# Image to columns on one core: all 72 plane copies on VectorE, none on ScalarE

## Chip, cores and metric

One core of a Trainium2 chip (trn2). The metric is the device time of one execution in microseconds (us), lower is better. Each kernel was run several times; a run is fast or slow, and only fast runs are compared.

## The reference

`x` is 16 x 64 x 32 x 32 in fp32, the window 3 x 3. For each of the 30 x 30 positions the patch of 64 x 3 x 3 values becomes a column:

```python
cols = np.zeros((batch, c * kernel_size * kernel_size, h_out * w_out), dtype=np.float32)
for b in range(batch):
    col_idx = 0
    for i in range(h_out):
        for j in range(w_out):
            patch = x[b, :, i:i + kernel_size, j:j + kernel_size].copy()
            cols[b, :, col_idx] = patch.ravel()
            col_idx += 1
```

No arithmetic is done: 4.19 MB go in and 33.18 MB come out, each input value in up to nine shifted copies.

## The kernel before

Each of 128 partitions holds 8 channels (CPP = 8) of one image. Three loads bring them in; for each channel nine copies of 30 x 30 elements, one for each shift (ki, kj), build the output in SBUF; five stores take it out: channel 0, channel 1, then pairs 2-3, 4-5, 6-7. The tile of a pair has two buffers, so pair 4-5 waits until the stores of channels 0 and 1 have landed (31.85 us; VectorE's copies start at 31.97), and pair 6-7 until that of pair 2-3 has (50.97; 51.09). Of every five copies two go to ScalarE.

```python
# (cut: views, pools, and the load helper on the SP queue)
    cuts = [0, H, 200, CPP * H]
    first = load(nc.sync, cuts[0], cuts[1])
    bulk = load(nc.sync, cuts[1], cuts[2])
    load(nc.sync, cuts[2], cuts[3])

    on_act = (False, True, False, True, False)
    n = 0
    for c in range(0, CPP, 2):
        out_tile = out_pool.tile([P, 2, KK, HO, WO], x.dtype, name="out_tile")
        for s in range(2):
            for kk in range(KK):
                ki, kj = divmod(kk, K)
                src = in_tile[:, c + s, ki : ki + HO, kj : kj + WO]
                dst = out_tile[:, s, kk]
                if on_act[n % len(on_act)]:
                    nc.scalar.copy(out=dst, in_=src)
                else:
                    nc.vector.tensor_copy(out=dst, in_=src)
                n += 1
            if c == 0:
                st = nc.sync.dma_start(
                    out=out_v[:, s],
                    in_=out_tile[:, s].rearrange("p kk i j -> p (kk i j)"),
                )
                if s == 0:

                    tc.add_manual_dep(
                        st.ins,
                        bulk.ins.name,
                        mybir.DependencyInfo(
                            mybir.DependencyClass.Sync, mybir.DependencyReason.DATA
                        ),
                        reason="the store follows the bulk of the loads",
                    )
        if c > 0:
            nc.sync.dma_start(
                out=out_v[:, c : c + 2].rearrange("p c n -> p (c n)"),
                in_=out_tile.rearrange("p c kk i j -> p (c kk i j)"),
            )
```

(After this the first load is moved ahead of the start barrier, in both kernels alike.)

Of the kernel before, what the change touches and what calls it, by code (L numbers as in the profile page):

```python
# [1 line left out]

# [3 lines left out]


def _im2col(ctx, tc, x, K, out):


    nc = tc.nc
    P = nc.NUM_PARTITIONS

    B, C, H, W = x.shape
    HO = H - K + 1
    WO = W - K + 1
    KK = K * K
    assert out.shape == (B, C * KK, HO * WO)
    CPP = B * C // P
    assert CPP * P == B * C and C % CPP == 0 and CPP % 4 == 0  # L20

    x_v = x.rearrange("b (cp c2) h w -> (b cp) (c2 h w)", c2=CPP)
    out_v = out.rearrange("b (cp c2 kk) n -> (b cp) c2 (kk n)", c2=CPP, kk=KK)

    in_pool = ctx.enter_context(tc.tile_pool(name="in_pool", bufs=1))
    out_pool = ctx.enter_context(tc.tile_pool(name="out_pool", bufs=2))

    ctx.enter_context(tc.manual_schedule())

    in_tile = in_pool.tile([P, CPP, H, W], x.dtype, name="in_tile")  # L30
    in_flat = in_tile.rearrange("p c h w -> p (c h w)")

    def load(queue, r0, r1):

        return queue.dma_start(
            out=in_flat[:, r0 * W : r1 * W], in_=x_v[:, r0 * W : r1 * W]
        )

    cuts = [0, H, 200, CPP * H]
    first = load(nc.sync, cuts[0], cuts[1])  # L40
    bulk = load(nc.sync, cuts[1], cuts[2])
    load(nc.sync, cuts[2], cuts[3])


    on_act = (False, True, False, True, False)
    n = 0
    for c in range(0, CPP, 2):
        out_tile = out_pool.tile([P, 2, KK, HO, WO], x.dtype, name="out_tile")
        for s in range(2):
            for kk in range(KK):  # L50
                ki, kj = divmod(kk, K)
                src = in_tile[:, c + s, ki : ki + HO, kj : kj + WO]
                dst = out_tile[:, s, kk]
                if on_act[n % len(on_act)]:
                    nc.scalar.copy(out=dst, in_=src)  # L55
                else:
                    nc.vector.tensor_copy(out=dst, in_=src)  # L57
                n += 1
            if c == 0:
                st = nc.sync.dma_start(  # L60
                    out=out_v[:, s],
# [17 lines that stand above are left out]
    return first  # L79


def kernel(
    tc: tile.TileContext,
    x: bass.AP,
    kernel_size: bass.AP,
    out: bass.AP,
):
    with ExitStack() as ctx:
        first = _im2col(ctx, tc, x, int(kernel_size), out)


    tc.close()
    tc.compile()  # L93
    blocks = tc.nc.main_func.blocks
    load = first.ins
    home = next(b for b in blocks if any(i.name == load.name for i in b.instructions))
    home.instructions = [i for i in home.instructions if i.name != load.name]
    head = list(blocks[0].instructions)
    at = next(
        k  # L100
        for k, i in enumerate(head)
        if i.engine == load.engine and type(i).__name__ == "InstDrain"
    )
    head.insert(at, load)
    blocks[0].instructions = head


# [1 line left out]
_INS = ['x', 'kernel_size']  # L109
_OUTS = [((16, 576, 900), 'float32')]  # L110

_NUMBERS = {'kernel_size': 3}


# [26 lines left out]
```

## Time and profile before

| | before |
|---|---|
| time, median of 3 runs at first | 91.44 us (91.39 to 91.49) |
| span of the profiled run (that run took 91.84 us) | 90.1 us |
| VectorE busy / ScalarE busy | 23.5 us / 26.2 us |
| DMA queue, share of 16 engines' time | 97.0% |

Read it as a kernel bound by its transfers: both copy engines are idle three quarters of the time, and the DMA queue is not. The prediction below shows the lines behind this table.

### The profile page before, as it was taken

The numbers are of one execution on the slowest core, as the hardware profiler recorded it, in microseconds if no ns is written. First come the engines' busy times: TensorE is split into PE (matmuls) and PEld (weight loads), VectorE is DVE, ScalarE is ACT, GpSimd is POOL, SyncE is SP. The second block draws the span as 40 slices with busy tenths as digits, with TensorE's granted clock in tenths as the row PEclk, the third lists the DMA queues.
The fourth block names the chain that finished last, engine by engine and source line by source line (L and its number), as shares of the span: only waits on it lengthen the run. The fifth ranks groups of instructions, "written<-read, shape, count | busy, mean of one in ns | idle before, by whom it ended". The sixth has DMA issues, their size and how long they took to land.

```text
span 90.1 us, 140 instructions
## 1 busy us (share of the span) xinstructions
DVE 23.5 (26%) x43; ACT 26.2 (29%) x30; POOL 0.2 (0%) x4
## 2 busy tenths in 40 slices
DVE  0380399970000089600000399300000000000000
ACT  5391399940000089920000399300000000000000
POOL 0000000000000000000000000000000000000000
DMA  5999899999599999993799999999999999947990
GB/s 129 486 382 449 360 518 446 460 460 446 259 460 460 691 460 432 460 432 173 345 460 460 460 460 460 460 460 460 460 460 460 460 432 460 403 201 345 460 460 0
DMA packets 1152, 37.37 MB, mean 415 GB/s; under 512 B 128, under 2 KB 128, under 8 KB 384
## 3 DMA queue, kind: packets, MB, share of 16 engines
q1 hardware_dynamic: 1152, 37.37, 97.0%
HBM read 4.19 MB, written 33.18 MB: 415 GB/s over the span
## 4 chain that ended last, share of the span: by engine, by line
DMA 45%; DVE 16%; DVEq 1%; issue 0%; SPq 0%
DMA out_dram<-out_tile 35%; DVE out_tile L57 16%; DMA in_tile<-in_x_dram 11%; DVEq L93 1%; DVEq L57 0%; SPq L75 0%
## 5 line engine op out<-in xcount | busy, mean ns | idle before, releaser
L55 ACT COPY out_tile<-in_tile 128x900 f32<-128x900 f32 x29 | 24.9, 938 | 30.1 <-DMA out_dram<-out_tile 25.3
L57 DVE COPY out_tile<-in_tile 128x900 f32<-128x900 f32 x43 | 23.5, 624 | 33.6 <-DMA out_dram<-out_tile 26.0
L55 ACT ACT_TABLE_LOAD x1 | 1.3, 1283 | 0.8 <-PEq L122 0.8
L122 POOL MEMSET const-bfloat16-1.0<- 128x1 bf16 x1 | 0.1, 102 | 0.0
L122 POOL MEMSET const-uint8-127<- 128x1 uint8 x1 | 0.1, 102 | 0.0
L122 POOL MEMSET const-float32-0.0<- 128x1 f32 x1 | 0.1, 99 | 0.2 <-issue 0.2
L122 POOL MEMSET const-float32-1.0<- 128x1 f32 x1 | 0.1, 99 | 0.0
## 6 DMA issues: line engine op xcount, KB each, us to landing
out_dram<-out_tile SPq DMA_DIRECT2D x3, 8100.0 KB, 31.3
out_dram<-out_tile SPq DMA_DIRECT2D x2, 4050.0 KB, 14.9
in_tile<-in_x_dram SPq DMA_DIRECT2D x1, 2688.0 KB, 9.6
in_tile<-in_x_dram SPq DMA_DIRECT2D x1, 896.0 KB, 11.4
in_tile<-in_x_dram SPq DMA_DIRECT2D x1, 512.0 KB, 3.6
```

Source lines behind the costliest of these rows:

```text
L55: nc.scalar.copy(out=dst, in_=src)
L57: nc.vector.tensor_copy(out=dst, in_=src)
L93: tc.compile()
L122: nc = _bacc.Bacc("TRN2", target_bir_lowering=False, num_devices=1)
```

## The change

The intent is a simpler program: VectorE alone does all the copies, so that ScalarE, with its table load (1.28 us in the page), is not used at all. The price is a VectorE that works longer and stores that are issued later.

```diff
--- before.py
+++ after.py
@@ -41,21 +41,15 @@
     bulk = load(nc.sync, cuts[1], cuts[2])
     load(nc.sync, cuts[2], cuts[3])
 
-
-    on_act = (False, True, False, True, False)
-    n = 0
     for c in range(0, CPP, 2):
         out_tile = out_pool.tile([P, 2, KK, HO, WO], x.dtype, name="out_tile")
         for s in range(2):
             for kk in range(KK):
                 ki, kj = divmod(kk, K)
-                src = in_tile[:, c + s, ki : ki + HO, kj : kj + WO]
-                dst = out_tile[:, s, kk]
-                if on_act[n % len(on_act)]:
-                    nc.scalar.copy(out=dst, in_=src)
-                else:
-                    nc.vector.tensor_copy(out=dst, in_=src)
-                n += 1
+                nc.vector.tensor_copy(
+                    out=out_tile[:, s, kk],
+                    in_=in_tile[:, c + s, ki : ki + HO, kj : kj + WO],
+                )
             if c == 0:
                 st = nc.sync.dma_start(
                     out=out_v[:, s],
```

## The prediction

With the comparison goes the reason why the stores could not run faster: 434 GB/s is what they ran at, not a ceiling that was shown, so "does not permit" means at that rate. Against contention the measured intervals of 19.1 to 19.2 us remain. The "some 1.2 us" from issue to first bytes is an estimate from one load: issued at 0.00, its first packet starts at 1.01 and the sixteenth at 1.35. The 938 ns under the rivals are one ScalarE copy in the page (mean of 29); the "at most 0.1 to 0.2 us" there is a guess of mine that nothing above works out. The 31.9 us before which the store issued at 19.74 "could not begin moving" are the landing on the slowest DMA engine: that store's first packet starts at 30.76, and the store ahead lands on its 16 engines from 31.15 to 31.85; so it began to move up to 1.1 us earlier than the sentence says.

> **What bounds the kernel now.** I began with the busy shares and the DMA queue of the page:
>
> ```profile
> DVE 23.5 (26%) x43; ACT 26.2 (29%) x30; POOL 0.2 (0%) x4
> ...
> q1 hardware_dynamic: 1152, 37.37, 97.0%
> ```
>
> VectorE (DVE) and ScalarE (ACT) each work about a quarter of the 90.1 us span; the single DMA queue moves 37.37 MB and its packets fill 97.0% of what 16 DMA engines have in that span. No copy engine is near its limit; the transfer of 4.19 MB in and 33.18 MB out nearly is. A share is only an average, so next I looked for moments at which the DMA queue had nothing to do because a copy was late. For that I need issue and landing of each store. The groups of DMA issues and the timeline give them:
>
> ```profile
> out_dram<-out_tile SPq DMA_DIRECT2D x3, 8100.0 KB, 31.3
> out_dram<-out_tile SPq DMA_DIRECT2D x2, 4050.0 KB, 14.9
> ...
> DMA to landing us min/median/max: 11.7/31.2/32.1
> ```
>
> ```profile
> 3.61 3.48 ACT L55 COPY out_tile<-in_tile 128x900 f32<-128x900 f32 x4 [1.54 <-DMA in_tile<-in_x_dram]
> 3.61 2.78 DVE L57 COPY out_tile<-in_tile 128x900 f32<-128x900 f32 x5 [3.61 <-DMA in_tile<-in_x_dram]
> 10.43 8.54 ACT L55 COPY out_tile<-in_tile 128x900 f32<-128x900 f32 x10 [3.35 <-DMA in_tile<-in_x_dram]
> 10.43 9.23 DVE L57 COPY out_tile<-in_tile 128x900 f32<-128x900 f32 x17 [4.04 <-DMA in_tile<-in_x_dram]
> 10.50 3.67 SPq L60 DMA_DIRECT2D out_dram<-out_tile  x2
> 19.74 0.33 SPq L75 DMA_DIRECT2D out_dram<-out_tile  x1
> ...
> 31.97 5.47 DVE L57 COPY out_tile<-in_tile 128x900 f32<-128x900 f32 x10 [12.31 <-DMA out_dram<-out_tile]
> 38.82 18.68 SPq L75 DMA_DIRECT2D out_dram<-out_tile  x2
> 51.07 6.01 ACT L55 COPY out_tile<-in_tile 128x900 f32<-128x900 f32 x7 [12.28 <-DMA out_dram<-out_tile]
> 51.09 6.01 DVE L57 COPY out_tile<-in_tile 128x900 f32<-128x900 f32 x11 [13.66 <-DMA out_dram<-out_tile]
> ```
>
> (Each row: start, duration, engine; in brackets the idle time before and what ended it.) The five stores go out at 10.50, 13.82, 19.74, 38.82 and 57.17 us. With the latencies 11.7 and 18.0 for the two single-channel stores, and 31.2, 31.3 and 32.1 for the three of two channels, they land at 22.2, 31.9, 51.0, 70.1 and 89.3. A store of 8.29 MB therefore lands every 19.1 us, that is 8.29 / 19.1 = 434 GB/s, although it spends over 31 us "in flight": the first 12 or so of those it stands behind the store before. The last load is issued at 1.18 and lands 11.4 later, at 12.6; five stores at that rate need 33.18 MB / 434 GB/s = 76.5 us, and 12.6 + 76.5 = 89.1 against 89.3 seen. The store stream has no hole of any size from 12.6 us on. The remaining 0.8 us to 90.1 is the end of the program.
>
> One view misleads here. The chain that ended last gives DVE 16% of the span:
>
> ```profile
> 10.43 9.24 DVE out_tile L57 x17
> ...
> 19.74 31.24 DMA out_dram<-out_tile
> ...
> 51.09 0.63 DVE out_tile L57
> ```
>
> It follows the last compute instruction back (its list ends at 57.10), and calls the 17 copies before the store at 19.74 part of the path. But that store could not begin moving before the one ahead of it landed at 31.9. Those copies are hidden.
>
> [...] The stretches between landings agree: 31.9 to 51.0 holds 6.9 us of copies on both engines and took 19.1 us, 51.0 to 70.1 holds 6.4 us and took 19.1, and 70.1 to 89.3 holds none and took 19.2.
>
> **The change, part by part.** It removes 29 ScalarE copies (24.9 us busy) and the table load (1.3 us), and adds 29 copies to VectorE. The compiled order shows nothing else: the same three loads and five stores on SP with the same buffer waits, less the wait for ScalarE; VectorE has 72 copies in the order of the code.
>
> VectorE's pace comes from the timeline: 17 copies take 9.23 us, and with 0.624 for the first the other 16 take (9.23 - 0.624)/16 = 0.538 each; the group of 10 gives (5.47 - 0.624)/9 = 0.538 too. So consecutive copies overlap a little, and n copies in a row take 0.624 + (n - 1) x 0.538: 4.93 us for the 9 of one channel, 9.77 for the 18 of a pair, 14.61 for 27. I take the starts from before, since they are set by loads and landings, and add:
>
> - Channel 0, from 3.61: done at 8.54 (before 7.09). Its store waits for the bulk load at 10.43 anyway: issued at 10.50, unmoved, with 1.9 us to spare.
> - Channel 1, from 10.43: done at 15.36, so its store goes out at about 15.4 instead of 13.82. The store ahead lands at 22.2. The first load shows some 1.2 us between issue and the first bytes (issued at 0.00, no DMA activity before 1.0), so anything issued by 21.0 leaves no hole: 5.6 us to spare.
> - Channels 2 and 3, straight after: done at 10.43 + 14.61 = 25.04 (before 19.7). Needed by 31.9 - 1.2 = 30.7: 5.6 us to spare.
> - Channels 4 and 5, when the first buffer is free at 31.97: done at 41.74 (before 38.8). Needed by 49.8: 8 us to spare.
> - Channels 6 and 7, from 51.09: done at 60.86 (before 57.1). Needed by 68.9: 8 us to spare.
>
> So copies of 29 x 0.538 = 15.6 us more on VectorE make four of five stores 1.6 to 5.3 us later at issue, and none later at landing. The sum on the path is 0. On the other side the table load (0.79 to 2.07) ended before the first data at 3.61, and the dropped semaphore wait is 17 ns in SP's record for each store; both were off the path, so the saving is 0 as well. VectorE ends up busy 4.93 + 14.61 + 2 x 9.77 = 39.1 us, 43% of the span.
>
> **The rivals.**
> *VectorE becomes the bound.* For it: it loses all help and its work grows by two thirds. Against it: a pair of channels takes 9.77 us and the DMA queue 19.1 us to drain one; a copy would have to take (19.1 - 1.2)/18 = 1.0 us before the queue ran dry in the steady part. If the copies nevertheless took 938 ns apiece with no overlap, channels 1 to 3 would end at 10.43 + 27 x 0.938 = 35.8 and leave a hole of about 5 us: 96.5 us. The 624 ns of 43 copies, 619 to 630, speak plainly against it.
> *The start gets later.* The beginning is where there is least slack: channel 0 ends 1.45 us later. Were the bulk load's landing not the gate, this would move everything, to 92.9. But it is, by 1.9 us; and even past 10.43, the last load keeps the queue supplied to 12.6.
> *Copies and transfers disturb each other.* VectorE would now copy from 10.4 to 25 without a pause, while loads and stores run. If 39 us of overlap cost 1% of DMA rate, that is +0.4 us, 91.8. The equal 19.1 to 19.2 us with and without copies speak against it.
> *Faster through less work.* No ScalarE instructions, no table load, one semaphore less. It could only shorten the beginning or end, both set by SP's own loads and last store; at most 0.1 to 0.2 us, 91.3.
>
> **Range and chances.** The time before is 91.44, from 91.39 to 91.49, and the sum of the parts is 0, so I predict 91.4. The range has to cover what the sum leaves out,[...] and the last two rivals: 91.1 to 91.8. Two per cent faster would be 89.6, which the rate of 434 GB/s does not permit with these bytes; two per cent slower is 93.3, and needs a hole of 1.8 us where the smallest margin behind a store is 5.6. I give 0.01 to faster, 0.02 to slower, 0.97 to the same.
>
> **What would show it right or wrong.** Right: VectorE x72, about 39 us busy, 624 ns each; stores issued near 10.5, 15.4, 25.1, 41.8 and 60.9, with latencies that shrink by as much as the issue moved (from 18.0 to about 16.5, from 31.2 to 26, from 31.3 to 28.3, from 32.1 to 28.4), landings unmoved, DMA share still about 97%. Wrong: a landing interval well over 19.1 us (contention), a copy time away from 624 ns or a pace away from 0.538, an issue of the first store after 10.5, or a DMA share under 95% with a hole between two stores.

## The result, and the profile after

The changed kernel takes 92.20 us (median of 6 runs, 92.12 to 92.42), the kernel before 91.50 (6 runs, 91.39 to 91.53). The ratio is 1.0084, 95% interval 1.007 to 1.0099. A ratio in this text is the mean time of one kernel's fast runs over that of the other's fast runs of the same rounds, so it is not quite the ratio of the medians. Executions over 1.5% slower than the fastest of the same kernel are left out of the means. "Within 2%" came true, but the change is clear of noise, 0.7 us, and 92.20 lies outside the stated 91.1 to 91.8. The prediction of the number was wrong.

What was said of the copies and the issues came true nearly to the digit. The page of the changed kernel, shares and queues, then its timeline (start, duration, engine; idle time before in brackets):

```profile
span 90.5 us, 128 instructions
...
DVE 39.1 (43%) x72; POOL 0.2 (0%) x4
...
q1 hardware_dynamic: 1152, 37.37, 96.5%
q14 instruction: 1, 0.01, 0.0%
```

```profile
3.44 4.93 DVE L49 COPY out_tile<-in_tile 128x900 f32<-128x900 f32 x9 [3.44 <-DMA in_tile<-in_x_dram]
10.44 14.61 DVE L49 COPY out_tile<-in_tile 128x900 f32<-128x900 f32 x27 [2.07 <-DMA in_tile<-in_x_dram]
10.50 5.24 SPq L54 DMA_DIRECT2D out_dram<-out_tile  x2
25.08 36.14 SPq L69 DMA_DIRECT2D out_dram<-out_tile  x3
31.96 9.77 DVE L49 COPY out_tile<-in_tile 128x900 f32<-128x900 f32 x18 [6.91 <-DMA out_dram<-out_tile]
51.09 9.77 DVE L49 COPY out_tile<-in_tile 128x900 f32<-128x900 f32 x18 [9.37 <-DMA out_dram<-out_tile]
```

4.93, 14.61, 9.77 and 9.77 us of copies, 39.1 us in all: as summed. The stores go out at 10.50, 15.40, 25.08, 41.75 and 60.89. They land at 22.2, 31.8 and 51.0, as before, and then at 70.5 and 89.6 instead of 70.1 and 89.3. So nothing was lost until 51 us, 0.4 us came in between 51.0 and 70.5, and it stayed.

One line is new, and its row in the page is easy to pass over: beside the queue of the kernel's own transfers there is a queue q14 of kind "instruction", with one packet. The DMA view of a stretch of 0.2 us of the changed kernel shows when it ran (packets are counted where they start):

```profile
DMA packets 1, 0.01 MB, mean 41 GB/s; under 512 B 0, under 2 KB 0, under 8 KB 0
...
q14 instruction: 1, 0.01, 9.7%
```

That is the stretch from 57.3 to 57.5 us: the only packet that starts in it is this one, 41 GB/s x 0.2 us = 8.2 KB; the record says 8192 bytes, start 57.39, 309 ns. From its kind I take it for a fetch of program text, and call it the fetch below; what it carries the trace does not show. The page of the kernel before has no such row. (Every packed trace also holds at least five such packets of 8192 bytes before the span; they end before the kernel's first transfer, in the kernel before at -7.92 us against 1.01 and in the changed one at -8.01 against 1.02, so only later ones are counted here.)

Why can one packet of 0.3 us move the end of a kernel with 1152 packets? Because a store has landed only when all 16 DMA engines have (in the changed kernel the copies of channels 6 and 7 start at 51.09, after the last engine's increment for store 2-3 at 50.98 and not after the median one's at 50.41), and each engine has a fixed amount to move: 64 data packets of this kernel, by the packet sizes in the trace. None is taken over by another engine: followed as described below, each of the 16 has its 24 store packets of 64,800 bytes in every trace. I worked the next table out of the trace: each store's semaphore gets one increment from each DMA engine, and the lag is how far the last of the 16 comes after the median one.

| lag of the slowest DMA engine, us | store 2-3 (lands near 51) | store 4-5 (near 70) | store 6-7 (near 89) |
|---|---|---|---|
| before | 0.51 | 0.51 | 0.50 |
| changed | 0.57 | 0.95 | 0.96 |

The median engines have not moved: 50.41, 69.55 and 88.68 in the changed kernel, 50.47, 69.61 and 88.75 before. One engine alone fell back. Following each engine's store packets by the continuity of their ends (mine, worked out from the trace; packets of 64,800 bytes follow one another every 2.39 us), an engine that was less than 0.05 us behind the median at 55 us is 0.25 behind one packet later and 0.91 behind after the next, and remains there. The packet that started at 54.77 took 2.63 us and the one at 57.70 took 2.75, against a median of 2.39; the fetch lies between them. Before, no packet of a store took over 2.44 us.

The span follows: median engine + lag + 0.81 us of program end. For the changed kernel 88.68 + 0.96 + 0.81 = 90.45, for the profiled run before 88.75 + 0.50 + 0.81 = 90.06. That explains 0.4 us. The other 0.3 us are in the profiled run before itself, which took 91.84 us and not 91.5; whether a run of 91.5 us has a smaller lag is for the control runs.

What asks for this packet these two traces do not show. They show it with 72 VectorE instructions and not with 43, on a queue of its own, and they show its cost on one engine: it runs from 57.39 to 57.70 us, and the store packet that took 2.75 us starts at 57.70. That VectorE's longer list brings it is a theory, which the runs have to try.

### The profile page after: what moved, and what is told of

Read it like the earlier page. It is cut to its first block, busy times and chain, and to the rows that moved or that the text cites. A ratio compares the mean times of both kernels' runs of the same rounds, so it can differ in the third digit from the quotient of the medians.

```text
span 90.5 us, 128 instructions
## 1 busy us (share of the span) xinstructions
DVE 39.1 (43%) x72; POOL 0.2 (0%) x4
## 3 DMA queue, kind: packets, MB, share of 16 engines
q1 hardware_dynamic: 1152, 37.37, 96.5%
## 4 chain that ended last, share of the span: by engine, by line
DMA 39%; DVE 26%; DVEq 1%; issue 0%
DMA out_dram<-out_tile 29%; DVE out_tile L49 26%; DMA in_tile<-in_x_dram 11%; DVEq L87 1%; DVEq L49 0%
## 5 line engine op out<-in xcount | busy, mean ns | idle before, releaser
L49 DVE COPY out_tile<-in_tile 128x900 f32<-128x900 f32 x72 | 39.1, 623 | 21.8 <-DMA out_dram<-out_tile 16.3
## 6 DMA issues: line engine op xcount, KB each, us to landing
out_dram<-out_tile SPq DMA_DIRECT2D x3, 8100.0 KB, 28.7
```

The lines of the kernel that those rows point to most:

```text
L49: nc.vector.tensor_copy(out=out_tile[:, s, kk], in_=in_tile[:, c + s, ki : ki + HO, kj : kj + WO],)
```

## The experiments

The theory: 29 more instructions bring VectorE's list past some boundary, and with it comes one more packet of kind "instruction", the fetch; it falls on one DMA engine, whose share of the stores ends later. The rivals, none of which needs a fetch: stores issued later cost something (late issue), longer VectorE work disturbs transfers (contention), a program without ScalarE starts or ends more slowly (ScalarE's absence), each VectorE instruction costs a little.

### Controls: both kernels again, three times in all

Edit: none. Runs c1_before_again and c2_after_again, and c3_after_third in a later set.

> Control: the kernel before, unchanged, so that its trace can be read twice. All theories expect a ratio of 1.00 (0.998 to 1.002) and 91.4 to 91.55 us. The first trace of it came from a run of 91.84 us, slower than all six timed runs, so its spans may have hidden part of the difference: I expect spans near 89.7 us here, no packet of the queue of kind instruction during the kernel, and the last store's slowest engine less than 0.5 us behind its median engine.

> Control: the changed kernel again. All theories expect about 92.2 us, a ratio of 1.007 to 1.010. Fetch theory ([...]the 8192-byte packet delays one DMA engine's stream of store packets): again an instruction packet at about 57 us, and the landing of the store in flight then at least 0.3 us later behind the median engine than that of the store before it. Rivals: nothing that needs such a packet.

> Control on another chip or at another time, since the runs of the kernel before spread from 91.53 to 92.27 us in the first set: the changed kernel, ratio 1.005 to 1.009; instruction packet near 57 us.

Measured: before again 91.70 us median (91.47 to 92.77), ratio to before 1.0003 (0.9959 to 1.0046), span 89.7, no q14 row. Changed again 92.26 (92.05 to 92.72), ratio 1.0056 (1.0024 to 1.0088), packet at 57.63; and a third time 92.20 (92.09 to 92.50), ratio 1.005 (1.0016 to 1.0083), packet at 57.66. These sets scattered more than the first: the kernel before went from 91.53 to 92.27 in the first set of controls and from 91.36 to 92.15 in the second (fast runs). So a ratio alone says less here than the trace. Two expectations missed: the 91.70 us lies above 91.4 to 91.55, and the 1.0056 of the changed kernel's first control below 1.007 to 1.010; the packets, the spans and the lags came as expected. These sets and all later ones ran on one chip.

The second trace of before answers the question of the 0.3 us. Its median engine lands the last store at 88.66, its slowest only 0.21 behind, and 88.66 + 0.21 + 0.81 = 89.68, the span. That run took 91.47 us, as those of the first round did (91.39 to 91.53), so their lags too were near 0.2, by estimate; the first profiled one had 0.5, which was there already when the bulk load landed (0.55). In the three traces of the changed kernel the lag is 0.95 or more. 0.95 - 0.21 = 0.74 us agrees with the difference that the timed runs of the first round show, 0.70.

### The kernel before, with 29 instructions more

Run e1_before_pad29. On purpose it does work that no one needs; the output is right.

```diff
+    pad_tile = in_pool.tile([P, 29], x.dtype, name="pad_tile")
+    for k in range(29):
+        nc.vector.memset(pad_tile[:, k : k + 1], 0.0)
     return first
```

> The kernel before with 29 one-element memsets on VectorE behind its last copy, so that VectorE has as many instructions as in the changed kernel while copies, issues of stores and ScalarE stay as before. Fetch theory: 92.1 to 92.3 us, ratio about 1.008, an instruction packet during the last two stores. Late-issue theory (stores issued 1.6 to 5.3 us later cost something), contention theory (39 us of VectorE copies beside transfers) and ScalarE-absence theory (a program without ScalarE instructions starts or ends more slowly): all three expect 91.4 to 91.55 us, ratio 1.000.

Measured: 92.27 us median (91.98 to 92.66), ratio 1.0052 (1.0022 to 1.0083). The timeline of its end, and the DMA view of 57 to 58 us:

```profile
51.14 6.01 ACT L55 COPY out_tile<-in_tile 128x900 f32<-128x900 f32 x7 [12.30 <-DMA out_dram<-out_tile]
51.16 6.01 DVE L57 COPY out_tile<-in_tile 128x900 f32<-128x900 f32 x11 [13.68 <-DMA out_dram<-out_tile]
57.12 0.43 DVE L81 MEMSET pad_tile<- 128x1 f32 x29
57.24 0.33 SPq L75 DMA_DIRECT2D out_dram<-out_tile  x1
```

```profile
q1 hardware_dynamic: 16, 1.04, 243.5%
q14 instruction: 1, 0.01, 1.9%
...
out_dram<-out_tile SPq DMA_DIRECT2D x1, 8100.0 KB, 32.4
```

ScalarE works, copies and issue of the last store (57.24) are those of the kernel before, VectorE has 0.4 us of extra work behind everything, and yet the kernel is as slow as the changed one (the ratio is under the expected 1.008, as the controls' is; the time is the expected one): the packet is there at 57.39, and the lag goes from 0.67 to 0.95. So none of late issue, contention and ScalarE's absence is needed for the loss.

### All copies on VectorE, in 45 instructions

Runs e2_after_merged and, in the later set, e7_after_merged_again. For the three later pairs one instruction copies both channels.

```diff
-        for s in range(2):
+        for s in range(2 if c == 0 else 0):
             (nine copies of one channel and its store, as before)
+        if c > 0:
+            for kk in range(KK):
+                ki, kj = divmod(kk, K)
+                nc.vector.tensor_copy(
+                    out=out_tile[:, :, kk],
+                    in_=in_tile[:, c : c + 2, ki : ki + HO, kj : kj + WO],
+                )
```

> All copies on VectorE, none on ScalarE, but for the three later pairs one instruction copies both channels of a pair: 18 + 27 = 45 VectorE instructions instead of 72, with the same elements and nearly the same issue times of the stores[...]. Fetch theory: no instruction packet, 91.4 to 91.6 us, ratio 1.000. Late-issue, contention and ScalarE-absence theories: as the changed kernel, about 92.2 us, ratio 1.008.

> The merged kernel (all copies on VectorE in 45 instructions) a second time, for a narrower interval. Fetch theory: 0.4 to 0.7 us below the changed kernel of the same rounds, ratio to the kernel before 0.998 to 1.003, no instruction packet before the last store has landed. Late issue, contention or the absence of ScalarE: ratio as the changed kernel.

Measured: 91.63 us (91.55 to 92.60; expected up to 91.6), ratio 1.0009 (0.9966 to 1.0052), then 91.58 (91.48 to 92.66, 7 runs), ratio 0.9986 (0.995 to 1.0021). The page's groups of the first of the two (busy us, mean ns of one, idle before) and its only row of a queue:

```profile
L71 DVE COPY out_tile<-in_tile 128x1800 f32<-128x1800 f32 x27 | 27.4, 1090 | 17.6 <-DMA out_dram<-out_tile 17.6
L49 DVE COPY out_tile<-in_tile 128x900 f32<-128x900 f32 x18 | 9.9, 623 | 5.3 <-DMA in_tile<-in_x_dram 5.3
```

```profile
q1 hardware_dynamic: 1152, 37.37, 97.1%
```

37.2 us of copies on VectorE, no ScalarE, stores issued late, no packet, no loss. So none of the three rivals is sufficient either. (It is the second set that decides: its interval ends at 1.0021, below the changed kernel's; that of the first reaches 1.0052.) This kernel needs one engine less than the kernel before and takes the same time; that it beats it is not shown.

One caution came with it. The profiled run of e7 was that kernel's slowest, 92.66 us with a span of 90.9, without a fetch: its slowest DMA engine was 1.17 us behind when the bulk load landed and still 1.00 behind at the end. So the loads alone can put an engine as far back as a fetch does. Of the 19 timed runs in these sets of kernels without a fetch, c1, e2 and e7, three took over 92.5 us (92.77, 92.60, 92.66); of these only the last was traced. The expectation of this run holds for its median, not for the run that was profiled.

### The same kernel with 15 instructions more

Run e8_merged_pad15, in the same set as e7 and c3.

```diff
 (the merged kernel)
+    pad_tile = in_pool.tile([P, 15], x.dtype, name="pad_tile")
+    for k in range(15):
+        nc.vector.memset(pad_tile[:, k : k + 1], 0.0)
     return first
```

> The merged kernel with 15 one-element memsets on VectorE behind its last copy: 60 VectorE instructions, beyond the boundary that lies above 51 and at or below 58. Only the number of instructions differs from the merged kernel, not a copy nor the issue of a store. Fetch theory: an instruction packet at about 61 to 63 us and the time of the changed kernel, 0.4 to 0.7 us above the merged one. Every rival: the time of the merged kernel.

Measured: 92.53 us (92.20 to 92.89), ratio to before 1.0087 (1.005 to 1.0124), 0.95 us over the median of the merged kernel in the same rounds. Its timeline's end and the DMA view of 57 to 58 us:

```profile
50.83 9.15 DVE L71 COPY out_tile<-in_tile 128x1800 f32<-128x1800 f32 x9 [9.99 <-DMA out_dram<-out_tile]
59.92 0.23 DVE L82 MEMSET pad_tile<- 128x1 f32 x15
```

```profile
q1 hardware_dynamic: 12, 0.78, 181.9%
q14 instruction: 1, 0.01, 1.9%
```

With 60 instructions the fetch is there and the time with it; only 0.23 us of work on an idle engine was added. Two parts of the expectation missed. The loss of 0.95 us is more than the expected 0.4 to 0.7, and 0.33 more than the changed kernel's in the same rounds; the traced run is the fastest of the six (92.20, lag 0.97), so what the slower ones had besides is open. And the packet came at 57.36, not at 61 to 63, before the first of the added instructions ran (59.92), so it was there before VectorE's execution had come to them. An instruction of VectorE's list that is recorded as begun while earlier ones still run is in the changed kernel's trace: the drain at the end of its program begins at 54.44 us, while copies run to 60.86. Whether the list was ahead here is not shown: in this run's trace the drain begins at 60.04.

### Where the boundary is

Runs e3_before_pad8, e4_before_pad15 and e5_before_pad22: as e1, with 8, 15 and 22 memsets instead of 29, one look each.

> The kernel before with 8 one-element memsets behind VectorE's last copy: 51 VectorE instructions of the kernel (43 and 45 had no instruction packet in earlier runs, 72 had one). Fetch theory as a step[...]: either no instruction packet and a span of 89.7 to 90.3 us, or one near 57 us and 90.3 to 90.9 us; nothing in between and no second packet. From the time of the packet in the changed kernel (57.4 us, about 12 copies into the last pair, so near the 66th copy), I expect none here. A theory in which each further VectorE instruction costs a little would give about 0.15 us over the kernel before, without a packet.

> As the run with 8 memsets, with 15: 58 VectorE instructions. Fetch theory: I expect no packet (the boundary lies near 60 to 66 by the time of the packet), span 89.7 to 90.3 us; if there is one, the boundary lies below 58. Cost per instruction: about 0.3 us over before, no packet.

> As the run with 8 memsets, with 22: 65 VectorE instructions. Fetch theory: near the boundary; a packet near 57 us and a span of 90.3 to 90.9 us if the boundary is below 65, and otherwise neither. Cost per instruction: about 0.4 us over before, no packet.

Measured: with 51 instructions no packet while stores run; with 58 and 65 one each, at 57.99 and 57.33. The DMA view of 91 to 95 us of the first shows where its fetch went:

```profile
q14 instruction: 1, 0.01, 0.5%
```

It is at 93.69, after the last store has landed at 90.95 and after the span's 91.8 us. The boundary lies above 51 and at or below 58 instructions of the kernel, not at 60 to 66 as I had expected from the time of the packet; an instruction list that is read ahead of execution would explain that miss, but no trace shows it. The spans (91.8, 91.1 and 90.4 us) miss the expected ones in the first two and cannot be compared: the loads were disturbed in them. In the run with 8 memsets the bulk load landed at 12.11 us instead of 10.4 and the last load at 14.25 instead of about 12.5; the store of channel 0 waits for the bulk load, and every engine's stores were 1.6 us later; the one run of the kernel before that went with these took 94.01 us. The lags can be compared: 0.72, 0.72, 0.72 for the last three stores without the fetch, 0.85, 1.02, 1.03 and 0.57, 0.88, 0.89 with it. It is a step, not a cost per instruction.

### ScalarE's list

Run e6_before_actpad43: 43 copies of one element on ScalarE behind its last copy.

```diff
+    for k in range(43):
+        nc.scalar.copy(out=pad_tile[:, k : k + 1], in_=in_tile[:, 0, 0, k % 32 : k % 32 + 1])
     return first
```

> The kernel before with 43 one-element copies on ScalarE behind its last copy, so that ScalarE has 72 instructions beside its table load and VectorE still 43. If the fetch belongs to each engine's own instruction list and both engines' lists begin alike, an instruction packet appears near 57 to 65 us and the span is 90.3 to 90.9 us. If only VectorE does this, or only VectorE's copies matter, no packet and 89.7 to 90.3 us.

Measured: a packet at 61.97 us, so ScalarE's list does it too: its 30 instructions in the kernel before gave none, 73 gave one; the place between was not narrowed further. DMA view of 60 to 64 us:

```profile
q1 hardware_dynamic: 17, 1.10, 63.9%
q14 instruction: 1, 0.01, 0.5%
```

The span, though, was 90.1, under what I expected: here the fetch fell on an engine that was 0.17 us ahead of the median and ended 0.47 behind, while another was 0.7 behind from the loads (reconstructed as above; by the semaphores the lag stays at 0.61). This fetch put its engine 0.64 us back, less than the 0.9 of VectorE's; why is open. In this run, then, the fetch did not set the end, since another engine was last.

### The boundary crossed at the start

Run e9_after_front60: the changed kernel, 60 memsets ahead of its first copy, 132 instructions.

```diff
+    pad_tile = in_pool.tile([P, 60], x.dtype, name="pad_tile")
+    for k in range(60):
+        nc.vector.memset(pad_tile[:, k : k + 1], 0.0)
+
     for c in range(0, CPP, 2):
```

> The changed kernel with 60 one-element memsets on VectorE ahead of its first copy (132 VectorE instructions), which run before the first data arrive at about 3.4 us. Fetch theory: the boundary is crossed at the start, so the packet appears at about 1 to 4 us; since the DMA queue is never empty from 1 us on, the engine that carries the fetch should stay behind to the end, and the time be that of the changed kernel, ratio 1.005 to 1.009 to the kernel before, not more although there are 60 instructions more. If a fetch at the start can be absorbed[...], ratio 1.000 to 1.003. A cost per instruction would make it 1.013 or more.

Measured: 92.28 us median (fast runs 92.13 to 92.30, and one slow run of 93.73), ratio 1.0054 (1.0021 to 1.0087). Timeline of the start, and the DMA view of 6 to 7 us:

```profile
0.85 1.72 DVE L46 MEMSET pad_tile<- 128x1 f32 x60 [0.85 <-PEq L120]
3.53 4.93 DVE L53 COPY out_tile<-in_tile 128x900 f32<-128x900 f32 x9 [0.96 <-DMA in_tile<-in_x_dram]
```

```profile
q1 hardware_dynamic: 24, 0.52, 123.4%
q14 instruction: 1, 0.01, 1.9%
```

One packet again, at 6.30 us (I expected 1 to 4), during the loads; the lag of the slowest engine is 0.77 at the store of channel 0 and 0.75 at the last. In time and in number 60 instructions more cost nothing over the changed kernel. At the landing of the bulk load, at 10.85 us instead of 10.4, the lag was 1.14. As the store of channel 0 waits for that load, its median landing is 21.88 us instead of 21.64: about 0.25 us passed to all engines, and the 0.75 that one was left with stayed for the 67 us that follow. So a fetch this early isn't absorbed: all five fast runs took 92.13 us or more. That all of the lag is the fetch's is not shown, since loads alone left 1.17 in e7.

### All of it in one view

Lags of the slowest DMA engine, in us, from each trace:

| kernel | VectorE instructions | fetch at us | lag, stores 2-3 / 4-5 / 6-7 | median us of the timed runs |
|---|---|---|---|---|
| before (first profile) | 43 | none seen | 0.51 / 0.51 / 0.50 | 91.50 |
| before again | 43 | none seen | 0.19 / 0.21 / 0.21 | 91.70 |
| merged | 45 | none seen | 0.37 / 0.36 / 0.36 | 91.63 |
| merged again | 45 | none seen | 0.99 / 1.01 / 1.00 (its slowest run) | 91.58 |
| before + 8 | 51 | 93.69, after the stores | 0.72 / 0.72 / 0.72 | one look |
| before + 15 | 58 | 57.99 | 0.85 / 1.02 / 1.03 | one look |
| merged + 15 | 60 | 57.36 | 0.36 / 0.95 / 0.97 | 92.53 |
| before + 22 | 65 | 57.33 | 0.57 / 0.88 / 0.89 | one look |
| before + 29 | 72 | 57.39 | 0.67 / 0.95 / 0.96 | 92.27 |
| changed | 72 | 57.39 | 0.57 / 0.95 / 0.96 | 92.20 |
| changed again | 72 | 57.63 | 0.71 / 1.09 / 1.09 | 92.26 |
| changed, third | 72 | 57.66 | 0.58 / 0.94 / 0.95 | 92.20 |
| changed, 60 ahead | 132 | 6.30 | 0.75 / 0.75 / 0.75 | 92.28 |
| before + 43 on ScalarE | 43 | 61.97 | 0.59 / 0.61 / 0.61 | one look |

Of the 35 fast timed runs of kernels whose trace has a fetch during the stores or loads none was below 91.98 us; the kernels without one had fast runs down to 91.36. VectorE's fetch sets a floor, since in all eight traces that have one within the span the last engine ends 0.75 to 1.09 behind; without it the lag, and the time, varies with how the loads went.

## Why the prediction was right or wrong

**What bounds the kernel: right.** The store stream has no hole, before or after: the median engine lands the last store at 88.75 and 88.68 us. The stores ran at 434 GB/s (8.29 MB every 19.1 us); that they could run no faster was not shown.

**VectorE's pace, its 39.1 us, the five issue times and the first three landings: right.** The latencies of the last two stores were to be 28.3 and 28.4 us; both are 28.7. These 0.4 and 0.3 us were the sign of error that the prediction itself had named, a landing interval over 19.1 us, here 19.5 between 51.0 and 70.5; but it had tied that sign to contention. (One reading was off without effect: between 51.0 and 70.1 the kernel before had 6.0 us of copies on each engine, not 6.4.)

**"The compiled order shows nothing else: the same three loads and five stores", and from it "The sum on the path is 0": wrong.** This is the step that failed. The compiled order did not list the packet of queue q14 that the trace shows at 57.39 us. The change turned 43 VectorE instructions into 72, across a boundary between 51 and 58, and added one fetch to a resource that the prediction had itself found full (97.0%). The term that was put at 0 measures 0.9 us on one DMA engine, and 0.7 us at the end in the first round, because an engine about 0.2 us behind is the last one otherwise.

**The table load and ScalarE's absence, put at 0: right.** The merged kernel has neither and takes the time of the kernel before (ratio 1.0009, then 0.9986).

**The rivals.** VectorE as the bound, a later start and contention did not happen. "Faster through less work" did not either. One argument against the later start does not hold, though: that past 10.43 "the last load keeps the queue supplied to 12.6". That is the slowest DMA engine; the median one is done with the loads at 12.04. In the five traces whose bulk load landed at 10.66 us or later (10.66, 10.85, 10.95, 11.07 and 12.11), the median landing of the first store came later with it (21.72, 21.88, 21.99, 22.15 and 23.18, against 21.57 to 21.68 in eight of the nine others). So the bulk load, for which the store of channel 0 waits, may land no later than about 10.55 us (21.6 less the 11.05 between the two landings in those five), by estimate: 0.1 us after its landing in the changed kernel (10.42). This is the tightest place, though it did not move here. The right rival, more instructions as more traffic (one packet of 8192 bytes), was not on the list.

**The range: too narrow.** It allowed 0.4 us for what the sum leaves out. The kernel before alone went from 91.36 to 92.77 us over its fast runs later.

**What stays open.** Why the loads leave one DMA engine behind by different amounts from run to run: 0.2 to 1.3 us at the landing of the bulk load, and 2.3 in the worst, the run with 8 memsets, of which 0.72 was left at its last three stores. Why the fetch is served near 57.4 us in kernels whose VectorE stands at quite different instructions then: if it is asked for after the wait that ends near 51 us, some 6 us pass, of which the traces show nothing; this is argued only. And the fetch's full size: VectorE's puts its engine 0.9 us back, which at the 64,800 bytes in 2.39 us of a store packet would be some 24 KB by estimate, while the one recorded packet has 8 KB and 0.31 us.

## What to carry to other kernels

When a change adds instructions to an engine, count them, and look for a row of kind "instruction" among the queues, with a packet of 8192 bytes: here it came within the span past a boundary between 51 and 58 instructions of VectorE. In this kernel, whose DMA queue filled 97.0% of its engines' time before the change, one such packet put one engine 0.9 us back. The slowest of the 16 ends the kernel (89.64 us in the changed one, the median 88.68), so what counts of that delay is the part that makes its engine the last: 0.7 us in the first round, and 0.36 to 0.69 us by medians of fast runs in the later ones, but nothing to be seen in the one look at ScalarE's fetch (span 90.1 us), which had another engine last. Fewer and larger instructions (45 instead of 72) removed the packet here. A DMA share near 97% is a mean: when the end moves with no hole to be seen, compare the last engine's landing with the median one's.
